# An MLP block on one Trainium2 core: the first w1 block loaded and scaled by halves of its columns, four pairs of x strips opened on it, a warm-up on the identity, two looks moved behind copies

## The chip, the cores and the metric

The kernel runs on one core of a Trainium2 chip. The metric is the device time of one execution in microseconds (us), as the median of several runs. The engines are TensorE (PE in the profile; PEld is its weight load), VectorE (DVE), ScalarE (ACT), GpSimd (POOL) and SyncE (SP), which here only issues transfers. Each engine works its instructions off in its own fixed order and waits for semaphores of the others.

## The reference

```python
# x (8, 1024, 1024), w1 (1024, 4096), w2 (4096, 1024), all float32
h = x @ w1
h = 0.5 * h * (1 + np.tanh(np.sqrt(2 / np.pi) * (h + 0.044715 * h ** 3)))
return (h @ w2).astype(np.float32)
```

## The kernel before, in words

x is taken as 8192 rows of 1024, cut into 64 strips of 128 rows; two strips are a pair (32 pairs). All products run on float16 operands that were scaled first. A strip is loaded (`load_x`), looked at by ScalarE, which sums its absolute values (`look_x`), given a scale by two tiny VectorE instructions (`scale_x`), cast (`cast_x`, on ScalarE, VectorE or GpSimd) and turned: eight 128x128 transposes on TensorE into PSUM, and a copy to the tile `xT` (`turn_x_pe`).

w1 is cut by columns into four blocks r of 2 x 512 columns. A block is a 2 x 2 arrangement of sub-blocks B11, B12, B21, B22 (upper or lower 512 rows; left or right 512 columns, 2048 apart). Each block comes in eight loads n of 512 KB (`load_w1`), two for each sub-block, in the order B11, B21, B12, B22. Each load is looked at for its largest magnitude (`look_w1`: on VectorE a reduction, on ScalarE a sum), `widest_w1` joins the looks, `scale_w1` spreads the result over all partitions with one TensorE transpose (the tile `rows`, L157) and takes its reciprocal, and `cast_w1` casts. Block 0 has two scales of its own before they are joined: NR for its left half (loads 0 to 3), NR + 1 for its right half (loads 4 to 7). `join_w1` and `even_w1` bring the two to one scale later, when block 0 is used in the other form.

The first half of the reference, x @ w1 and the gelu, goes in two forms. The opening of block 0 for the first six pairs is plain: a *quarter* (class `Plain`, `quarter`) is one 128 x 512 piece of h, given by pair k, strip half and column side s, and takes eight TensorE products, four with B11 (or B12) and four with B21 (or B22). There are 24 quarters; their list puts s = 0 of the pairs below OPEN first, then s = 1 of these, then the other pairs. Between the first four and the last four products of a quarter `between(p)` puts the next strip's turn and the looks and casts of what comes next. From then on a pair and block is a *unit* (class `Quad1`) of seven products of half size on sums of sub-blocks (`sum_x`, `sum_w1`), with partial results copied out of PSUM by ScalarE (L503, L513, L522) and added by VectorE. A gelu is one ScalarE activation out of PSUM with a factor per row (`up`), then a multiplication by GpSimd to float16 (L173, tile `g`) and a store to DRAM. The second half, the product with w2, follows with 26 products of 256 columns for each pair; it is untouched.

What sets the order: everything is recorded by hand, engine by engine, in the order of the source (`manual_schedule`); no scheduler moves anything. `plan(u, slot, ...)` puts a background step at a slot of unit u, `early(p, ...)` behind quarter p. The opening itself is written out in lines 793 to 874. Transfers from SP go on one hardware queue and are issued in order, with eight landing semaphores in rotation, so the ninth issue waits until the first has landed. w1 blocks 1 to 3 are loaded on GpSimd's queue, so these issues stand in GpSimd's order between its casts.

The places that the change and the prediction touch: the opening (L793 to L874), `load_w1`, `look_w1`, `widest_w1`, `join_w1`, `even_w1`, `cast_w1` (L267 to L323), `factors_of_block` (L250), `warm_up` (L410), `Out1` with its gelus (L421 to L458), and the plan of block 2's looks (L673 to L676). The opening's sequence before: load x0, w1 loads 0 to 3, x1 to x5, w1 loads 4 to 7, x6, x7; cast and turn x0; 14 warm-up products on the cast x0; looks at loads 0 to 3 (the last shared by VectorE and ScalarE); scale; eight more warm-up products; casts of loads 0 and 1 on VectorE, 2 and 3 on ScalarE; quarters, beginning with pair 0.

Of the kernel before, what the change touches and what calls it, by code (L numbers as in the profile page):

```python
# [8 lines left out]
F32 = mybir.dt.float32  # L9
# [4 lines left out]
P = 128  # L14
TINY = 1e-18
SPAN = 256.0


# [61 lines left out]
def kernel(  # L80
# [23 lines left out]
    LAST = 4  # L104
    OPEN = 3
    WARM = 14
    Q = O // 4
# [19 lines left out]
    w1c = small.tile([P, NR, 12], F32, name="w1c")  # L127
    w1a = small.tile([P, NR + 2], F32, name="w1a")
    w1m = small.tile([P, NR + 2], F32, name="w1m")
    w1i = small.tile([P, NR + 2], F32, name="w1i")  # L130
    w1j = small.tile([P, NR + 2], F32, name="w1j")
# [8 lines left out]
    rt = small.tile([P, T // P], F32, name="rt")  # L140
    up = small.tile([P, 2, 2 * FIRST], F32, name="up")
    ratio = small.tile([P, 2], F32, name="ratio")

# [99 lines left out]
    def factors(k0, k1, r):  # L243
# [4 lines left out]
        times(view(rs), xi[:, c], w1j[:, r:r + 1])  # L248

    def factors_of_block(k, block, eng):  # L250

        c, b = slice(2 * k, 2 * k + 2), slice(NR + block, NR + block + 1)
        times(up[:, block, c], xm[:, c], w1m[:, b], eng)
        times(rt[:, c] if block else rs[:, k, :, 0], xi[:, c], w1j[:, b], eng)

    def factors_of_pair(k):
        for h in range(2):
            times(us[:, k, h, :], w1m[:, :NR], xm[:, 2 * k + h:2 * k + h + 1])
            times(rs[:, k, h, :], w1j[:, :NR], xi[:, 2 * k + h:2 * k + h + 1])
        times(rt[:, 2 * k:2 * k + 2], xi[:, 2 * k:2 * k + 2], w1j[:, NR + 1:NR + 2])  # L260


# [4 lines left out]
    def load_w1(r, n, pool=wpool, tag="w"):  # L267
        b, half = BLOCKS[n // 2], n % 2
        row = (b in (B21, B22)) * HK * P + half * 2 * P
        col = (b in (B12, B22)) * I // 2 + r * N  # L270
        wraw[r, n] = pool.tile([P, 2, N], F32, name="wn", tag=tag)
        (G if r else nc.sync).dma_start(
            out=wraw[r, n],
            in_=w1[row:row + 2 * P, col:col + N].rearrange("(c p) n -> p c n", p=P),
        )

    def look_w1(r, n, eng=V, part=None):

        i = n + 2 * (n // 4) + (2 if part else 0)
        src, dst = wraw[r, n], w1c[:, r, i:i + 1]  # L280
        if part is not None:
            src = src[:, part:part + 1]
        src = src.rearrange("p c n -> p (c n)")
        if eng is S:
            junk = k2.tile([P, 2 * N], mybir.dt.bfloat16, name="junk", tag="k2")
            junk = junk[:, :src.shape[1]]
            S.activation(out=junk, in_=src, func=ACT.Abs, scale=1.0 / SPAN, accum_out=dst)  # L287
        else:
            absmax(dst, src)

    def widest_w1(r, block=None):

        c, src = (r, w1c[:, r, :]) if block is None else (NR + block, w1c[:, r, 6 * block:6 * block + 6])
        V.tensor_reduce(out=w1a[:, c:c + 1], in_=src, op=ALU.max, axis=AX.X)
# [8 lines left out]
    def inverse_w1(c, eng=V):  # L303
        times(w1j[:, c], w1i[:, c], 1.0 / SPAN, eng)

    def join_w1():

        V.tensor_tensor(out=w1m[:, :1], in0=w1m[:, NR:NR + 1], in1=w1m[:, NR + 1:], op=ALU.max)
        V.reciprocal(w1i[:, :1], w1m[:, :1])
        times(ratio, w1m[:, NR:], w1i[:, :1])  # L310
        V.tensor_copy(out=w1j[:, :1], in_=w1j[:, NR:NR + 1])

    def even_w1(b, half):
        t = w1set[0, b][:, 2 * half:2 * half + 2]
        block = b in (B12, B22)
        cast(G, t, t, ratio[:, block:block + 1])

    def cast_w1(r, n, eng):
        b, half = BLOCKS[n // 2], n % 2
        if (r, b) not in w1set:  # L320
            w1set[r, b] = wpool.tile([P, HK, N], F16, name="w", tag="w")
        c = r or NR + n // 4
        cast(eng, w1set[r, b][:, 2 * half:2 * half + 2], wraw.pop((r, n)), w1i[:, c:c + 1])  # L323

# [27 lines left out]
    def scale_w2():  # L352
        all_partitions(w2n, w2a)
        V.tensor_scalar_max(w2n, w2n, TINY)
        V.reciprocal(w2i, w2n)
        V.tensor_scalar(out=w2s, in0=w1m, scalar1=w2i, scalar2=None, op0=ALU.mult)

# [52 lines left out]
    def warm_up(t, n):  # L410
        warm = bank("pb")
        for _ in range(n):
            nc.tensor.matmul(  # L413
                warm[:, :N // 2], lhsT=t[:, :P], rhs=t[:, :N // 2],
                start=True, stop=True, skip_group_check=True,
            )
# [4 lines left out]
    class Out1:  # L421


        def begin(self, k, r):
# [6 lines left out]
            if not r and k < FIRST:  # L431
                self.u = [[up[:, s, c(h)] for s in range(2)] for h in range(2)]
            if k not in gd:
                gd[k] = dram.tile([2 * P, I], F16, name="gd", tag="gd")

        def e(self):
            return k2.tile([P, N], F32, name="e", tag="k2")

        def gelu_pair(self, half, s, src):
            e = self.e()  # L440
            S.activation(out=e, in_=src, func=ACT.Gelu_apprx_tanh, scale=self.u[half][s])
            if half not in self.g:
# [9 lines left out]
        def gelu(self, half, s, e, src):  # L452
            S.activation(out=e, in_=src, func=ACT.Gelu_apprx_tanh, scale=self.u[half][s])  # L453
            g = k1.tile([P, N], F16, name="g", tag="k1")
# [10 lines left out]
    class Plain(Out1):  # L465
        def __init__(self, k, r):
            self.begin(k, r)
            self.g = {}

        def quarter(self, half, s, which, between):  # L470
# [166 lines left out]
    for k in range(OPEN, FIRST):  # L637
        for h in range(2):
            c = 2 * k + h
            p = (6, 9, 12)[k - OPEN] + h  # L640
            early(p - 1, look_x, c)
            early(p, scale_x, c)
            early(p, cast_x, c, V)
            if h:
                early(p, factors_of_block, k, 0, V)
                early(p, factors_of_block, k, 1, G)
            if k > 3:
                early((2, 5)[k - 4], load_x, c, wpool, "w")
            early(4 * k - 2 + 2 * h - (k > 2), turn_x_pe, c, V if h else S)
# [7 lines left out]
    for n in range(8):  # L657
        early((3, 4, 6, 7, 8, 9, 10, 11)[n], load_w1, 1, n)
        early((7, 8, 10, 12, 12, 13, 14, 15)[n], look_w1, 1, n, S if n in (3, 5, 7) else V)
# [9 lines left out]
    for r in range(2, NR):  # L669
        u = (r - 1) * FIRST - 1  # L670
        for n in range(8):
            v = u - 1 + n // 2
            if r == 2:  # L673
                plan(*((4, 1), (4, 3), (5, 0), (5, 2))[n // 2], load_w1, r, n)
                look = ((5, 3), (5, 4), (6, 1), (6, 1), (6, 3), (7, 1), (7, 1), (7, 4))[n]
                plan(*look, look_w1, r, n, S if n % 2 else V)  # L676
# [110 lines left out]
    with tc.manual_schedule(  # L787
# [5 lines left out]
        load_x(0, wpool, "w")  # L793
        for n in range(4):
            load_w1(0, n)
# [4 lines left out]
        V.tensor_copy(out=identity16, in_=identity)  # L800
        for c in range(1, 2 * OPEN):
            load_x(c, wpool, "w")
        for n in range(4, 8):
            load_w1(0, n)
        for c in range(2 * OPEN, 8):
            load_x(c, wpool, "w")
        look_x(0)
        scale_x(0)
        cast_x(0, S)
        t = x16[0]  # L810
        turn_x_pe(0, S)
        warm_up(t, WARM)
        for n in range(3):
            look_w1(0, n)
        look_w1(0, 3, V, 0)
        look_w1(0, 3, S, 1)
        widest_w1(0, 0)
        look_x(1)
        scale_w1(NR)
        warm_up(t, 8)  # L820
        cast_w1(0, 0, V)
        inverse_w1(slice(NR, NR + 1), G)
        cast_w1(0, 1, V)
        cast_w1(0, 2, S)
        cast_w1(0, 3, S)
        scale_x(1)
        cast_x(1, V)
        for c in range(2, 5):
            look_x(c)
        factors_of_block(0, 0, G)  # L830
        plain = {k: Plain(k, 0) for k in range(FIRST)}
        quarters = [(k, 0, half, s) for s in range(2) for k in range(OPEN) for half in range(2)]
        quarters += [(k, 0, half, s) for k in range(OPEN, FIRST) for half in range(2) for s in range(2)]

        def between(p):
            if p == 0:
                turn_x_pe(1, V)
                scale_x(2)
                cast_x(2, V)
            elif p == 1:  # L840
                scale_x(3)
                turn_x_pe(2, V)
                cast_x(3, V)
                look_x(5)
                scale_x(4)
                cast_x(4, V)
                factors_of_block(1, 0, G)
            elif p == 2:
                turn_x_pe(3, V)
                look_w1(0, 4)  # L850
                look_w1(0, 5, S)
            elif p == 3:
                scale_x(5)
                cast_x(5, G)
                turn_x_pe(4, V)
                look_w1(0, 6)
                look_w1(0, 7, S)
                widest_w1(0, 1)
                factors_of_block(2, 0, G)
            elif p == 4:  # L860
                turn_x_pe(5, V)

        for p, (k, r, half, s) in enumerate(quarters):
            plain[k].quarter(half, s, ("pa", "pc")[p % 2], lambda: between(p))
            if p == 4:
                scale_w1(NR + 1)
# [51 lines left out]
```

## Time and profile before

| | |
|---|---|
| median of 3 runs | 1531.62 us (1531.59 to 1531.94) |
| the profiled execution's own time | 1532.23 us |
| its span, first to last instruction | 1530.4 us |
| ScalarE's start on x0 (its landing) | 4.59 us |
| TensorE's first instruction (turn of x0) | 7.36 us |
| TensorE's first product of a quarter | 12.96 us |
| looks at an x strip on ScalarE, first 60 us | 12, mean 1048 ns |
| 128x1024 casts of w on ScalarE, first 60 us | 8, mean 1145 ns |
| gelus of 128x512 out of PSUM (L441) | mean 687 ns |

The profile is of one execution. Its times count from the first instruction; the execution's own time is longer than the span by what lies around it. A timeline gives for each engine start, length and what ran, and in brackets the idle time ahead and what ended it. Products are pipelined, so a group's length has a tail of some 0.16 us that overlaps with the next group: eight products of 512 columns stand in the list with 1.89 us but begin 1.73 us apart from the next eight.

### The profile page before, as it was taken

Reading aid. Unit: us, or ns where it says so; the run is one execution under the profiler, and the core shown is the slowest. Engines: PE = TensorE matmul, PEld = TensorE weight load, DVE = VectorE, ACT = ScalarE, POOL = GpSimd, SP = SyncE. Lnnn points to the kernel's source line nnn. Section 1 sums busy time; section 2 is a strip of 40 time slices with the busy share of each in tenths; the row PEclk is TensorE's granted clock in tenths of the full one; section 3 lists DMA queues with packets and bytes.
Section 4 is the critical chain, followed back from the end, with each engine's and each line's share of the span. In section 5 each row is a group of like instructions: output and inputs, shape, how many; then the busy total and the mean of one; then the engine's idle time right before and its main releaser. Section 6 shows DMA issues by size and latency. Waiting matters only on the chain.

```text
span 1530.4 us, 28624 instructions
## 1 busy us (share of the span) xinstructions
PE 1518.0 (99%) x10388; PEld 1013.0 (66%) x10388; DVE 1179.4 (77%) x2406; ACT 736.5 (48%) x1307; POOL 475.6 (31%) x591
## 2 busy tenths in 40 slices
PE   7999999999999999999999999999999999999999
PEld 4444444444444444444458888888888888888888
DVE  6886788777876777574348888888888888888886
ACT  7878777777777777787662111111111111111111
POOL 5688554555666656554440000000000000000000
PEclk9999999999999999999999999999999999999999
DMA  9664988878778787875995767767866866866873
GB/s 357 230 196 133 299 273 290 253 237 239 213 241 270 220 262 226 252 200 131 285 275 135 144 135 135 144 139 132 156 130 130 163 133 122 163 135 130 150 143 79
DMA packets 459935, 293.94 MB, mean 192 GB/s; under 512 B 333968, under 2 KB 427152, under 8 KB 459792
## 3 DMA queue, kind: packets, MB, share of 16 engines
q1 hardware_dynamic: 456336, 279.52, 71.8%
q0 software_dynamic: 3456, 12.58, 2.5%
q8 instruction: 81, 1.33, 0.4%
q14 instruction: 62, 0.51, 0.1%
HBM read 96.99 MB, written 114.29 MB: 138 GB/s over the span
## 4 chain that ended last, share of the span: by engine, by line
PE 99%; DVE 1%; ACT 0%; DMA 0%; issue 0%; ACTq 0%
PE pa L401 52%; PE pc L401 31%; PE pb L401 14%; PE turned L212 0%; DMA xn<-in_x_dram 0%; DVE x L175 0%; PE pb L413 0%; DVE w L175 0%; DVE xT L219 0%; ACT x L171 0%; ACT junk L186 0%; ACT junk L287 0%; PE rows L157 0%; DVE xi L193 0%; DVE o L571 0%
## 5 line engine op out<-in xcount | busy, mean ns | idle before, releaser
L401 PEld LDWEIGHTS <-gs 128*128 128x128 f16 x4608 | 450.8, 98 | 53.1 <-DVE gs L167 0.2
L173 POOL TENSOR_SCALAR g<-e,rs 128x512 f16<-128x512 f32 x446 | 364.2, 826 | 285.7 <-ACT e L453 248.6
L401 PEld LDWEIGHTS <-xs 128*128 128x128 f16 x1952 | 191.0, 98 | 230.5 <-issue 0.9
L164 DVE TENSOR_TENSOR e<-pc,e 128x512 f32<-128x512 f32 x244 | 162.9, 686 | 204.2 <-ACT e L522 202.8
L401 PEld LDWEIGHTS <-xT 128*128 128x128 f16 x1656 | 161.2, 98 | 194.1 <-DVE xT L219 1.7
L401 PE MATMUL pa<-w,gs 128*128 128x256 f16 x2304 | 288.3, 273 | 0.0
L401 PE MATMUL pa<-w,xT 128*128 128x512 f16 x1072 | 254.4, 379 | 0.4 <-DVE w L175 0.3
L453 ACT ACTIVATE e<-e,us 128x512 f32<-128x512 f32 x366 | 251.2, 719 | 3.1 <-DVE e L164 3.1
L401 PE MATMUL pa<-w,xs 128*128 128x512 f16 x976 | 250.5, 379 | 0.6 <-ACT e L503 0.6
L401 PE MATMUL pc<-w,xs 128*128 128x512 f16 x976 | 250.5, 379 | 0.0
L401 PEld LDWEIGHTS <-gT 128*128 128x128 f16 x2048 | 200.4, 98 | 23.2
L575 ACT ACTIVATE o<-pa,vo 128x256 f32<-128x256 f32 x96 | 45.2, 471 | 332.5 <-PE pa L401 332.5
L401 PE MATMUL pc<-w,gs 128*128 128x256 f16 x1536 | 193.8, 273 | 0.0
L401 PE MATMUL pa<-w,gT 128*128 128x256 f16 x1024 | 132.7, 273 | 0.0
L401 PE MATMUL pb<-w,xT 128*128 128x512 f16 x488 | 125.3, 379 | 0.0
L571 DVE SCALAR_TENSOR_TENSOR o<-pc,vo,o 128x256 f32<-128x256 f32 x160 | 77.1, 482 | 57.8 <-PE pc L401 57.8
L513 ACT COPY e<-pa 128x512 f32<-128x512 f32 x122 | 71.4, 585 | 92.3 <-PE pa L401 83.9
L167 DVE TENSOR_TENSOR gs<-gT,gs 128x1024 f16<-128x1024 f16 x160 | 109.9, 687 | 1.2 <-DMA gT<-gd 1.2
L571 DVE SCALAR_TENSOR_TENSOR o<-pa,vo,o 128x256 f32<-128x256 f32 x192 | 92.2, 481 | 19.5 <-PE pa L401 19.3
L401 PE MATMUL pb<-w,gs 128*128 128x256 f16 x768 | 99.5, 273 | 0.0
L401 PE MATMUL pc<-w,gT 128*128 128x256 f16 x768 | 99.5, 273 | 0.0
L503 ACT COPY e<-pa 128x512 f32<-128x512 f32 x122 | 70.5, 578 | 50.7 <-PE pa L401 50.6
(104 smaller groups left out, 1436.6 us busy)
## 6 DMA issues: line engine op xcount, KB each, us to landing
gd<-g SPq DMA_DIRECT2D x500, 128.0 KB, 3.2
wn<-in_w_dram SPq DMA_DIRECT2D x72, 512.0 KB, 5.4
xn<-in_x_dram SPq DMA_DIRECT2D x64, 512.0 KB, 5.4
out_dram<-o SPq DMA_DIRECT2D x62, 512.0 KB, 4.0
w<-wd SPq DMA_DIRECT2D x25, 512.0 KB, 6.0
wn<-in_w_dram POOLq DMA_DIRECT2D x24, 512.0 KB, 6.3
wd<-wt SPq DMA_DIRECT2D x24, 512.0 KB, 4.2
gT<-gd SPq DMA_TRANSPOSE x128, 6.4
```

The costliest lines, as they stand in the source:

```text
L164: V.tensor_tensor(out=o, in0=a, in1=b, op=ALU.add)
L167: V.tensor_tensor(out=o, in0=a, in1=b, op=ALU.subtract)
L173: G.tensor_scalar(out=o, in0=i, scalar1=s, scalar2=1.0, op0=ALU.mult, op1=ALU.mult)
L401: nc.tensor.matmul(bank, lhsT=left(i), rhs=right[i], start=start and i == 0, stop=i == n - 1, skip_group_check=True,)
L453: S.activation(out=e, in_=src, func=ACT.Gelu_apprx_tanh, scale=self.u[half][s])
L503: S.copy(self.e11, self.pa)
L513: S.copy(self.e12, self.pa)
L571: V.scalar_tensor_tensor(out=o, in0=ps, scalar=v, in1=o, op0=ALU.mult, op1=ALU.add)
L575: S.activation(out=o, in_=ps, func=ACT.Copy, scale=v)
```

## The change

Block 0's first half (B11 and B21) is loaded by halves of its columns: loads 0 and 1 bring columns 0 to 255 of the upper and lower 512 rows (four row groups of 256 columns each), loads 2 and 3 columns 256 to 511. Each half has its own scale (columns NR + 2 and NR + 3 of the scale tiles), so the factor `up` has three versions, and a gelu over both halves is two activations of 256 columns. `join_halves` makes the common maximum for the factor behind the gelu. The first two quarters (pair 0) become four *eighths* of 256 columns; x1 is loaded between load 1 and load 2. OPEN goes from 3 to 4: x6 and x7 are loaded ahead of w1 loads 4 to 7, and s = 0 of four pairs comes ahead of s = 1. The 14 warm-up products on x0 become 52 of 128 columns on the identity ahead of x0's turn, and three ahead of the rows product, eight behind it and three ahead of x1's turn. In the opening x0 is cast by ScalarE as before, x5 and x7 by GpSimd, the others by VectorE; looks at w1 loads 4 and 6 are VectorE's, 5 and 7 ScalarE's, loads 1 and 3 shared, load 2 ScalarE's. Block 1's first two loads are one quarter later. Two of block 2's looks, loads 1 and 3, move in the plan from (5, 4) and (6, 1) to (6, 1) and (6, 4), which is behind the copies of unit 6.

```diff
-    OPEN = 3
-    WARM = 14
+    OPEN = 4
+    WARM = 52
...
+    def ups_of_block(k, eng):
+        c = slice(2 * k, 2 * k + 2)
+        for half in range(2):
+            times(up[:, half, c], xm[:, c], w1m[:, NR + 2 + half:NR + 3 + half], eng)
...
+        c, w = 2, N
+        if not r and n < 4:
+            c, w = HK, N // 2
+            row, col = n % 2 * HK * P, n // 2 * w
...
+    def join_halves():
+
+        V.tensor_tensor(
+            out=w1m[:, NR:NR + 1], in0=w1m[:, NR + 2:NR + 3], in1=w1m[:, NR + 3:], op=ALU.max
+        )
+        V.reciprocal(w1i[:, NR:NR + 1], w1m[:, NR:NR + 1])
...
+        def act(self, half, s, e, src):
+            u = self.u[half][s]
+            u = u if isinstance(u, tuple) else (u,)
+            w = N // len(u)
+            for i, scale in enumerate(u):
+                c = slice(i * w, (i + 1) * w)
+                S.activation(out=e[:, c], in_=src[:, c], func=ACT.Gelu_apprx_tanh, scale=scale)
...
+        def eighth(self, half, part, ps):
+
+            t = xT[self.k]
+            c = slice(part * N // 2, (part + 1) * N // 2)
+            for j, b in enumerate((B11, B21)):
+                product(
+                    ps[:, c], lambda n: t[:, half, j * HK + n, :],
+                    [w1set[0, b][:, n, c] for n in range(HK)], j == 0,
+                )
...
-        early((3, 4, 6, 7, 8, 9, 10, 11)[n], load_w1, 1, n)
+        early((4, 5, 6, 7, 8, 9, 10, 11)[n], load_w1, 1, n)
...
-                look = ((5, 3), (5, 4), (6, 1), (6, 1), (6, 3), (7, 1), (7, 1), (7, 4))[n]
+                look = ((5, 3), (6, 1), (6, 1), (6, 4), (6, 3), (7, 1), (7, 1), (7, 4))[n]
...
         load_x(0, wpool, "w")
-        for n in range(4):
+        for n in range(2):
+            load_w1(0, n)
+        load_x(1, wpool, "w")
+        for n in range(2, 4):
             load_w1(0, n)
...
-        for c in range(1, 2 * OPEN):
+        for c in range(2, 2 * OPEN):
             load_x(c, wpool, "w")
         for n in range(4, 8):
             load_w1(0, n)
-        for c in range(2 * OPEN, 8):
-            load_x(c, wpool, "w")
+        warm_up(identity16, WARM)
         look_x(0)
         scale_x(0)
         cast_x(0, S)
         t = x16[0]
+        look_w1(0, 0)
+        look_w1(0, 1, V, 0)
+        look_w1(0, 1, S, 1)
         turn_x_pe(0, S)
-        warm_up(t, WARM)
...
+        warm_up(t, 3)
+        widest_w1(0, 2)
+        look_x(1)
+        scale_w1(NR + 2)
+        warm_up(t, 8)
+        cast_w1(0, 0, V)
+        cast_w1(0, 1, V)
+        plain = {k: Plain(k, 0) for k in range(FIRST)}
+        pa, pc = bank("pa"), bank("pc")
+        plain[0].eighth(0, 0, pa)
+        look_w1(0, 2, S)
+        scale_x(1)
+        cast_x(1, V)
         look_w1(0, 3, V, 0)
         look_w1(0, 3, S, 1)
+        widest_w1(0, 3)
+        look_x(2)
+        warm_up(t, 3)
+        turn_x_pe(1, V)
+        scale_w1(NR + 3)
+        plain[0].eighth(1, 0, pc)
+        cast_w1(0, 2, V)
+        cast_w1(0, 3, S)
+        ups_of_block(0, G)
+        scale_x(2)
+        cast_x(2, V)
+        look_x(3)
+        join_halves()
+        inverse_w1(slice(NR, NR + 1), G)
+        plain[0].eighth(0, 1, pa)
+        turn_x_pe(2, V)
+        times(rs[:, 0, :, 0], xi[:, 0:2], w1j[:, NR:NR + 1], G)
+        plain[0].gelu(0, 0, plain[0].e(), pa)
+        look_x(4)
+        plain[0].eighth(1, 1, pc)
+        plain[0].gelu(1, 0, plain[0].e(), pc)
+        scale_x(3)
+        cast_x(3, V)
...
+            if p == 2:
+                turn_x_pe(3, V)
                 look_x(5)
                 scale_x(4)
                 cast_x(4, V)
                 factors_of_block(1, 0, G)
...
             elif p == 3:
+                turn_x_pe(4, V)
+                look_x(6)
+                look_x(7)
                 scale_x(5)
                 cast_x(5, G)
...
+                look_w1(0, 4)
             elif p == 4:
                 turn_x_pe(5, V)
+                scale_x(6)
+                cast_x(6, V)
+                factors_of_block(2, 0, V)
+                look_w1(0, 5, S)
+                look_w1(0, 7, S)
+            elif p == 5:
+                turn_x_pe(6, V)
+                scale_x(7)
+                cast_x(7, G)
+                look_w1(0, 6)
+                widest_w1(0, 1)
+            elif p == 6:
+                turn_x_pe(7, V)
+                factors_of_block(3, 0, V)
```

## Prediction

> **What bounds it now.** I read the page first, then TensorE's timeline and its waits in the first 80 us, then the chain of waits in order of time, then the other engines' timelines over the same stretch. The span is TensorE's work behind a head of 13 us.
>
> ```profile
> PE 1518.0 (99%) x10388; PEld 1013.0 (66%) x10388; DVE 1179.4 (77%) x2406; ACT 736.5 (48%) x1307; POOL 475.6 (31%) x591
> ...
> PE 99%; DVE 1%; ACT 0%; DMA 0%; issue 0%; ACTq 0%
> ```
>
> So only two things can change the time: when TensorE's useful work begins, and how long it then stands still. TensorE's timeline (start, length, what):
>
> ```profile
> 8.19 3.19 PE L413 MATMUL pb<-x 128*128 128x256 f16 x14
> 11.17 0.42 PE L157 MATMUL rows<-identity,w1a 128*128 128x128 f32 x1
> 11.44 1.24 PE L413 MATMUL pb<-x 128*128 128x256 f16 x8
> 12.96 1.25 PE L401 MATMUL pa<-w,xT 128*128 128x512 f16 x4 [0.28 <-DVE w L175]
> 14.68 0.62 PE L212 MATMUL turned<-identity,x 128*128 128x128 f16 x8 [0.46 <-DVE x L175]
> ...
> 31.07 1.89 PE L401 MATMUL pa<-w,xT 128*128 128x512 f16 x8
> ```
>
> L413 is warm-up; the first product starts at 12.96. The ninth quarter (s = 1, pair 0) starts at 31.07. Between lie 8 quarters of 8 x 0.216 = 1.73 us, 5 turns of 0.45 (8 transposes at 0.056) and a rows product, 0.11: 16.2 of 18.1 us, so 1.9 us of stalls. After 31.07 the engine is gapless but for 0.16 at 42.9 and one stall, which the waits (PE behind ACT e L503, 0.6) and ScalarE's timeline explain:
>
> ```profile
> 62.51 1.05 ACT L287 ACTIVATE junk<-wn 128x1024 bf16<-128x1024 f32 x1
> 63.45 0.19 ACT L287 ACTIVATION_READ_ACCUMULATOR junk<-wn 128x1 f32 x1
> 63.55 0.57 ACT L503 COPY e<-pa 128x512 f32<-128x512 f32 x1
> ```
> ```profile
> 62.52 1.03 PE L401 MATMUL pb<-w,xT 128*128 128x512 f16 x4
> 64.17 1.02 PE L401 MATMUL pa<-w,xs 128*128 128x512 f16 x4 [0.62 <-ACT e L503]
> ```
>
> The product at 64.17 was due at 62.52 + 0.86 = 63.39: 0.78 us lost, because a look at a w1 block stood ahead of the copy.
>
> **Part 1, the first product.** Unchanged: x0 lands at 4.57, its look, scale and cast end at 7.31. Six loads in, the trace's records of landing are 4.57, 5.89, 7.27, 8.62, 9.95, 11.23: 1.28 us per x strip (4 KB rows), 1.35 per w1 load (2 KB rows). The new w1 loads have the same bytes in 1 KB rows. The nearest 1 KB rows are the stores of g, 0.33 us apart for 128 KB behind each other, so 1.33 per 512 KB; a cost per packet, as from 1.28 to 1.35, would give 1.48. I take 1.37. Landing then: w 5.9 and 7.3, x1 8.6, w 9.95 and 11.3. The second load's half look on VectorE (0.69) ends at 8.0, on ScalarE behind cast x0 (0.63 + 0.19) at 8.05; widest 0.16; rows at 8.2. From rows to cast it took 0.83 (25.74 to 26.57), the cast 0.75: first product at **9.85, 3.1 us earlier**; the second half of it behind the second cast (0.67 on) at 10.5.
>
> **Part 2, the second half block.** ScalarE: copy xT of x0 to 9.05, look x1 to 10.2, look w to 11.2, half look to 11.95. VectorE: scale and cast x1 10.45 to 11.55 (0.38 + 0.75), half look to 12.15, widest 12.3, copy xT of x1 12.25 to 12.85, and w1m behind it; cast w from 13.4 to 14.15. ScalarE's cast waits behind look x2 (lands 12.55, done 13.6) and ends 14.7. TensorE: product 2 at 12.95, product 3 at 14.2 and 14.75, turn x2 15.2, product 4 15.65 to 16.55. At this state (two quarters, x1 and x2 turned) before stood at 18.5: 1.9 ahead.
>
> **Part 3, quarters 2 to 6.** Between two turns TensorE has 1.73 us; VectorE needs copy 0.61, scale 0.38, cast 0.75 and some 0.25 to and from PSUM: 2.0. So each turn waits about 0.2 (before: 0.17 to 0.34), and x5, cast on GpSimd in 1.12, about 0.55. Turns: x3 17.65, x4 20.05, x5 22.8, x6 25.15; TensorE is ready for x7 at 27.3.
>
> **Part 4, where x7 stands.** Its cast is on GpSimd, in order behind g of quarter 4 and the issue of the load of w1 block 1. That g waits for quarter 4's gelu, and ScalarE's order has looks at w1 loads 5 and 7 ahead of this gelu. Load 7 is now the last of the 16 first loads, which x7 was before (landing on record: 24.30); with four loads 0.02 longer, 24.4. What each step behind takes:
>
> ```profile
> 21.85 1.06 ACT L287 ACTIVATE junk<-wn 128x1024 bf16<-128x1024 f32 x1
> ```
> ```profile
> 22.77 1.12 POOL L173 TENSOR_SCALAR x<-xn,xi 128x1024 f16<-128x1024 f32 x1
> ...
> 24.51 0.69 POOL L173 TENSOR_SCALAR g<-e,rs 128x512 f16<-128x512 f32 x1
> 25.14 0.89 POOL L272 DMA_DIRECT2D wn<-in_w_dram  x1
> ```
>
> Look 24.4 to 25.45 (next start 1.04 on); two half gelus; no row has them. A 512 copy from PSUM took 0.578, a 256 one with a scale 0.471, a 512 gelu 0.687; 0.687 less 256 columns at 0.83 ns is 0.474, the second starting 0.38 behind the first (between 0.29, half the present pitch, and 0.57, no shorter than a whole one): to 26.3. g from 26.35, issue 0.64 on, cast 0.80 behind it (29.85 to 30.65 at the next issue): 27.8 to 28.95. **Turn x7 at 29.0, a new stall of 1.7.** Then 0.45, half a quarter 0.86, rows 0.11, quarter 7 1.73: the ninth quarter at 32.15. Before, 31.07 plus the turns of x6 and x7, which it does later, 2 x 0.45: 31.97. **The head ends 0.2 us behind**; all 3.1 are given back.
>
> **Part 5, the rest.** The two looks of block 2 go behind copies: the copy starts when its product ends, 61.66 + 1.03 = 62.69 on the old clock, and ends 63.26, ahead of 63.39. Next late is the copy behind the moved look (1.04 from 63.26, so 64.3; its product ends 64.4): no stall. **Minus 0.78** (0.6 to 0.78). The casts of w1 loads 5 to 7 end 32.45, 33.05 and 33.5 against needs of 32.6, 33.0 and 33.45: plus 0.1 (0 to 0.3). The 0.16 at 42.9 may go; I take 0. At nothing: twelve gelus in halves (0.18 each) under ScalarE's 52% idle time, the extra up factors (0.26 on GpSimd, 0.15 on VectorE), evening by columns (as many elements as before), GpSimd's loads of block 1 one slot later (looked at from about 33, landing about 33.5, used from 50). 52 warm-ups begin behind the identity's cast (1.6), at 0.107 end at 7.15, before x0.
>
> Sum: 0.2 - 0.78 + 0.1 = -0.5. The profiled execution took 1532.23 (span 1530.4 and 1.8 around it), so 1531.7; the median of the runs is 0.6 below it: **1531.1**.
>
> **The clock.** Before, products of 256 columns stand 0.213 apart until 11.8 us, 4.4 us after the first transpose at 7.36, then 0.109; the page's PEclk shows 9 throughout, so I go by spacing. New warm-ups start at 1.6, so 4.4 later is 6.0, before x0 is turned. Released after that, x0's turn and three warm-ups cost up to 0.4 + 0.3 more, rows come 0.6 later, and about 0.45 reaches the end. The Trainium skill, TensorE: Matmul & The Clock Gate, Part 1, says that the window of about 3.4 us is free-running, so that release falls anywhere from one to two windows after the start; by that it is estimated at 5.0 to 8.4, and the sum by its late end is 1531.55.
>
> **Rivals.**
> A: x7 is not held (the look at load 7 ends early, or g overtakes), so the stall is as at x5, 0.55: 1.15 better, and the half us of slack in Part 3 may count: 1529.6. For it: all upstream steps are ready. Against: every queue is in order. 0.13.
> B, slower: 1 KB rows move more slowly, and load 7 lands late. Place: ScalarE's look at load 7. Behind it each us is a us of the end, so the balance turns at a landing of 24.9. At 1.48 a load it is 24.85 (1531.55), at 1.7 25.75: 1532.4. For: 4 KB to 2 KB already costs 5%. Against: the stores of g. The Trainium skill, DMA: Bandwidth & Descriptors, Specifications, puts line rate at transfers from 512 B on; by that the landing is 24.3 and the sum 1531.0. 0.18.
> C, the warm-up on the identity does not do what it says, or the clock falls back: from 8.2 to 16.5 TensorE is busy some 60%. Not released until 11.8, as before: rows product about 0.9 and first product 1.6 later than at 9.85, about 1.1 at the end: 1532.2; falling back for one stretch of 3.4 us half-paced: 1.7, 1532.8. Against: before, 12.4 to 16.1 was busy 60% too, and its transposes stood 0.056 apart. 0.13.
>
> **Chances.** Forecast 0.51 (1530.5 to 1531.9), A 0.13, B 0.18, C 0.13, 0.05 for what I don't see. Range 1530.2 to 1533.0: it leaves out most of A and the far ends of B and C. 0.2% is 3.1 us, about what a measurement of this kernel can tell from no change. No case reaches it alone: faster 0.03 (A with all stalls of Part 3 gone), same 0.94, slower 0.03 (B and C together).
>
> **What would show it.** First product near 9.85, product 4 ending near 16.5; PE turned waiting near 27.3 to 29.0 with GpSimd's cast of x as releaser, behind an ACT look released by the DMA of wn; no PE wait on ACT e near 64. Wrong, if the turn of x7 starts before 28, if transposes at 7.4 stand 0.107 apart, or if the w1 loads land over 1.5 us apart.

## The result and the profile after

After: **1533.68 us** (median of 22 runs, 1532.97 to 1535.27) against 1531.84 before (22 runs, 1531.31 to 1532.32). The ratio is 1.0014, 95% interval 1.0007 to 1.002: slower by 1.8 us, 2.6 above the 1531.1 that was forecast and outside the range. The profiled execution of after took 1533.54, its span is 1531.8 (before 1532.23 and 1530.4).

On the page of after, the engine totals look as they did before. In the chain of work that ended last, DMA has 2% instead of 0, and GpSimd's `x`, its `wn` issue and its `g` are new, each below half a per cent.

```profile
PE 1521.4 (99%) x10449; PEld 1017.0 (66%) x10449; DVE 1180.4 (77%) x2417; ACT 740.0 (48%) x1321; POOL 473.9 (31%) x592
...
PE 98%; DMA 2%; POOL 0%; SPq 0%; DVE 0%; issue 0%
```

TensorE's timeline of after (start, length, what; idle time and its releaser in brackets):

```profile
1.64 4.96 PE L451 MATMUL pb<-identity 128*128 128x128 f16 x52 [1.64 <-DVE identity L858]
7.61 0.62 PE L213 MATMUL turned<-identity,x 128*128 128x128 f16 x8 [1.01 <-ACT x L172]
8.06 0.49 PE L451 MATMUL pb<-x 128*128 128x256 f16 x3
8.82 0.29 PE L158 MATMUL rows<-identity,w1a 128*128 128x128 f32 x1 [0.26 <-DVE w1a L312]
...
10.48 1.26 PE L438 MATMUL pa<-w,xT 128*128 128x256 f16 x8
...
16.39 1.04 PE L438 MATMUL pc<-w,xT 128*128 128x256 f16 x8
...
24.02 0.62 PE L213 MATMUL turned<-identity,x 128*128 128x128 f16 x8 [0.44 <-POOL x L174]
...
27.94 1.04 PE L438 MATMUL pa<-w,xT 128*128 128x512 f16 x4
30.99 0.62 PE L213 MATMUL turned<-identity,x 128*128 128x128 f16 x8 [2.02 <-POOL x L174]
...
34.15 1.98 PE L438 MATMUL pa<-w,xT 128*128 128x512 f16 x8
```

The reader sees the forecast's shape with other sizes. The first product starts 2.5 us before its old place (12.96), product 4 at 16.39, and TensorE is ready for x7 at 28.80 (27.94 and four products of 0.216). Then it stands still for 2.2 us (2.02 behind the modelled end of the last product). The ninth quarter starts at 34.15, where before it stood at 31.97 with as much work done: the head ends **2.2 us later**. From there to the end after needs 1531.8 - 34.15 = 1497.65, before 1530.4 - 31.97 = 1498.43: **about 0.8 less**, the size at which the two moved looks were priced (what it consists of stands under Part 5 below). 2.2 - 0.8 is the 1.4 by which the spans differ.

What held x7 is the chain of waits of after from 25 us on (start, length, what):

```profile
20.89 7.33 DMA gd<-g
28.22 0.01 issue
28.23 0.69 POOL g L174
28.93 0.84 POOL wn L286
29.76 0.05 issue
29.81 1.13 POOL x L174
30.95 0.05 issue
30.99 0.62 PE turned L213 x8
```

and ahead of it ScalarE's timeline of after:

```profile
26.26 1.06 ACT L302 ACTIVATE junk<-wn 128x1024 bf16<-128x1024 f32 x1 [1.29 <-DMA wn<-in_w_dram]
27.23 0.19 ACT L302 ACTIVATION_READ_ACCUMULATOR junk<-wn 128x1 f32 x1
27.32 0.82 ACT L483 ACTIVATE e<-pa,up 128x256 f32<-128x256 f32 x2
```

ScalarE waits 1.29 us for the last w1 load, looks at it, does the gelu of quarter 4; GpSimd does its g, issues a load, casts x7. All six steps are the forecast's, in its order. Load 7 landed at 26.18, not at 24.4. The first row of the chain names another releaser for this g, the store of an earlier one. It is the gelu, as the run with the looks later (below) shows: there the gelu ends at 27.25 and g starts at 27.34, 0.09 behind it as in after (28.14, 28.23), while the records of landing of that store come at 27.59 to 29.31.

**Why the last of the 16 lands 1.9 later than before's last.** The records of landing of the first 16 loads, in us:

| | x0 lands | first four w1 loads, each | 2 KB w1 loads | x strips | largest gap between two | last of the 16 |
|---|---|---|---|---|---|---|
| before | 4.57 | 1.32 to 1.38 (2 KB rows) | 1.35 to 1.36 | 1.26 to 1.29 | 1.38 | 24.30 |
| after | 4.81 | 1.41 to 1.50 (1 KB rows) | 1.31 to 1.37 | 1.27 to 1.33 | **2.43**, x5 to x6 | 26.18 |

So 0.24 are a later start (of this execution alone: in the other twelve profiles x0 lands at 4.34 to 4.62), about 0.45 are the 1 KB rows (four times 0.11), and 1.15 are one gap in front of x6 (2.43 less 1.28), which lands at 19.5. In that gap the transfers of after, from 16.5 to 17.5 us, show a queue other than the loads' (packets, MB, share of the time of 16 engines):

```profile
q1 hardware_dynamic: 104, 0.39, 96.9%
q8 instruction: 1, 0.02, 6.8%
```

One packet of 16 KB, with 6.8% of 16 engine-microseconds: it holds one of the 16 DMA engines for 1.09 us, from 16.71 on. It is TensorE fetching its next stretch of program, as the count below shows. The trace has sixteen records of landing for each load, and a load has landed with the last of them. Up to x5 the last comes at most 0.04 behind the one before it; from x6 to load 7 it comes 1.14 to 1.19 behind: fifteen of load 7's sixteen stand by 25.01, the last at 26.18. So one share of everything behind this packet is some 1.15 us late, and the other fifteen lose nothing. Before, the same fetch came at 25.0, when all 16 loads had landed, and no such lag is in their records (0.08 at most). The fetches follow the count of instructions: 81 packets on this queue for 20,898 products and weight loads of the page, one in 258; in each of the thirteen traces the median distance from one packet to the next is 253 to 260 of them. Some 220 to 245 of them are on record ahead of this fetch, in before by 25.0 and in after by 16.7: after issues 44 more warm-ups and, in place of two quarters, twice as many products of half the width, each with its weight load.

### The profile page after: what moved, and what is told of

Read it like the earlier page. It is cut to its first block, busy times and chain, and to the rows that moved or that the text cites. A ratio compares the mean times of both kernels' runs of the same rounds, so it can differ in the third digit from the quotient of the medians.

```text
span 1531.8 us, 28775 instructions
## 1 busy us (share of the span) xinstructions
PE 1521.4 (99%) x10449; PEld 1017.0 (66%) x10449; DVE 1180.4 (77%) x2417; ACT 740.0 (48%) x1321; POOL 473.9 (31%) x592
## 3 DMA queue, kind: packets, MB, share of 16 engines
q8 instruction: 81, 1.33, 0.4%
## 4 chain that ended last, share of the span: by engine, by line
PE 98%; DMA 2%; POOL 0%; SPq 0%; DVE 0%; issue 0%
PE pa L438 52%; PE pc L438 31%; PE pb L438 14%; DMA xn<-in_x_dram 1%; DMA gd<-g 0%; PE turned L213 0%; POOL x L174 0%; SPq L286 0%; POOL wn L286 0%; PE rows L158 0%; POOL g L174 0%; DVE o L627 0%; SPq L183 0%; SPq L504 0%
## 5 line engine op out<-in xcount | busy, mean ns | idle before, releaser
L438 PE MATMUL pa<-w,xT 128*128 128x512 f16 (+1 forms) x1080 | 254.8, 377 | 0.3
```

The costliest lines, as they stand in the source:

```text
L438: nc.tensor.matmul(bank, lhsT=left(i), rhs=right[i], start=start and i == 0, stop=i == n - 1, skip_group_check=True,)
```

## The experiments

Each kernel was timed in 11 runs beside 27 to 33 runs of before in the same batch; before's median was 1531.61, 1531.62 and 1531.66 in the three batches.

### Taking links out of the chain of x7

**The looks at loads 5 and 7 behind the gelu of quarter 4** (after, with this edit):

```diff
         elif p == 4:
-            look_w1(0, 5, S)
-            look_w1(0, 7, S)
         elif p == 5:
             ...
             cast_x(7, G)
             look_w1(0, 6)
+            look_w1(0, 5, S)
+            look_w1(0, 7, S)
```

> The changed kernel, but ScalarE's looks at w1 loads 5 and 7 stand one quarter later, behind the gelu of quarter 4. Theory (load 7 lands at 26.2 and holds ScalarE, and through it gelu, GpSimd's g, its load issue and the cast and turn of x7): the gelu no longer waits for the landing; next late are its factors, which VectorE writes behind the cast of x6 (26.4 to 26.75 in the changed kernel's trace), so it starts at 26.8 instead of 27.3 and x7's turn moves from 31.0 to 30.4: 0.55 us faster than the changed kernel, median 1533.1. Rival (the landing only happens to fall there, GpSimd's own queue is late): turn of x7 stays at 31.0, 1533.7. If the landing alone were the hold and nothing came next, the turn would come at 29.0 to 29.6 and the median at 1531.9.

Measured: 1533.30 (1532.31 to 1534.02), ratio 1.0011 (1.0002 to 1.002). Turn of x7 in its TensorE timeline:

```profile
30.10 0.62 PE L213 MATMUL turned<-identity,x 128*128 128x128 f16 x8 [1.44 <-POOL x L174]
```

The stall falls from 2.2 to 1.6, not to nothing: the look is one gate of quarter 4's gelu, and the next one is 0.6 us earlier, VectorE's factors of pair 2 behind the cast of x6. The forecast had only the first. (The turn is 0.9 earlier than in after; 0.3 of it is that TensorE was ready earlier, in an execution in which x0 landed at 4.38 and not at 4.81.)

**x7 cast on VectorE instead of GpSimd** (`cast_x(7, G)` to `cast_x(7, V)` in after):

> The changed kernel, but x7 is cast by VectorE instead of GpSimd, so that its turn waits for nothing of ScalarE's and GpSimd's queues. Theory: VectorE has x7's scale at 28.15, cast to 28.95, turn at 29.0 instead of 31.0; the stall of 2.0 goes but for 0.2, and the median comes to 1531.7 to 1531.9, the same as the kernel before. The look at load 6 starts 0.7 later and its result is still ahead of the rows product. Rival (something else, such as the scale of the right half behind load 7, takes the place): the ninth quarter moves less than 1 us and the median stays above 1532.8. Clock: if the stall of 2 us is what lets the clock fall back in the slower of the changed kernel's executions (granted clock 0.999 there), no execution shows 0.999 here; if the thin stretch from 8 to 16 us is, about a quarter of them still do.

Measured: 1533.05 (1531.80 to 1533.50), ratio 1.0007 (0.9998 to 1.0016). The stall at x7 falls from 2.2 to 0.6, but its TensorE and VectorE timelines show the next thing that is late:

```profile
29.78 0.62 PE L213 MATMUL turned<-identity,x 128*128 128x128 f16 x8 [0.44 <-DVE x L176]
...
32.13 1.90 PE L438 MATMUL pc<-w,xT 128*128 128x512 f16 x8 [0.58 <-DVE xT L220]
33.87 1.99 PE L438 MATMUL pa<-w,xT 128*128 128x512 f16 x8
```
```profile
28.54 1.18 DVE L176 TENSOR_SCALAR x<-xn,xi 128x1024 f16<-128x1024 f32 x1
29.64 1.20 DVE L151 TENSOR_REDUCE w1c<-wn 128x1 f32<-128x1024 f32 x1
30.95 0.16 DVE L312 TENSOR_REDUCE w1a<-w1c 128x1 f32<-128x6 f32 x1
31.38 0.69 DVE L220 COPY xT<-turned 128x1024 f16<-128x1024 f16 x1 [0.27 <-PE pa L438]
```

VectorE now casts x7 in 1.18 (0.75 for x6), and the copy of x7 stands behind the look at load 6 and the join. Half of the rival: something else took the wait's place, though a smaller one.

**x7 cast one quarter earlier on GpSimd**, ahead of quarter 4's g and of the load's issue:

```diff
         elif p == 4:
             cast_x(6, V)
+            scale_x(7)
+            cast_x(7, G)
             factors_of_block(2, 0, V)
             ...
         elif p == 5:
             turn_x_pe(6, V)
-            scale_x(7)
-            cast_x(7, G)
```

> The kernel after, with the scale and the cast of x7 put one quarter earlier, so that GpSimd casts x7 ahead of quarter 4's g and of the load's issue, and nothing of x7 waits for load 7; the looks stay. Theory (the turn of x7 waits for load 7 only through the order of three queues; all upstream steps are ready): GpSimd casts x7 from about 26.8 to 27.95, TensorE takes the turn when it is ready, near 28.8, with no wait over 0.3; the ninth quarter starts near 32.0 instead of 34.15, the span is about 1529.6, the median about 1531.2, some 0.5 under the kernel before beside it. Rival (the landing of load 7 itself is the bound, whatever the queues): rows or the casts of loads 4 to 7 take the wait over, the ninth quarter stays later than 33.3, and the median is above 1532.5.

Measured: 1531.84 (1531.42 to 1532.90), ratio 1.0001 (0.9992 to 1.001): the loss is gone. TensorE, then VectorE:

```profile
28.60 1.04 PE L438 MATMUL pa<-w,xT 128*128 128x512 f16 x4 [0.62 <-DVE xT L220]
29.48 0.61 PE L213 MATMUL turned<-identity,x 128*128 128x128 f16 x8
...
32.62 2.05 PE L438 MATMUL pa<-w,xT 128*128 128x512 f16 x8
```
```profile
26.86 1.10 DVE L242 TENSOR_SCALAR rs<-xi,w1j 128x2 f32<-128x2 f32 x1
27.87 0.68 DVE L220 COPY xT<-turned 128x1024 f16<-128x1024 f16 x1
```

x7 is turned without a wait, as the theory says; load 7 lands as late as ever (26.48) and the time no longer shows it, against the rival. But the ninth quarter stands at 32.62 and not at 32.0: a new wait of 0.6 for the copy of x6, because a product of 128x2 numbers ahead of it took 1.10 us (0.22 in after). It ends, at 27.96, with GpSimd's cast of x7 (26.79 to 27.94).

**Both, x7 ahead and the looks later:**

> As the run with x7 cast ahead, and the looks at loads 5 and 7 behind the gelu of quarter 4 as well. Theory: with x7 out of the queue, the gelu of quarter 4 has nobody who waits for it before its bank is wanted again, so this adds nothing: within 0.3 of the other run, ninth quarter near 32.0. Rival: the late gelu still holds a bank or a factor, and this is better by 0.5 or more.

Measured: 1532.30 (1531.96 to 1533.53), ratio 1.0005 (0.9996 to 1.0014). Both sides missed: it is 0.5 worse than x7 ahead alone. The looks, now later on ScalarE, end at 29.8 and hold `widest_w1` by 0.21, and again a small VectorE step beside GpSimd's g takes 0.79 (0.35 in after); the casts of loads 4 to 7 begin at 32.00 (31.74 there).

**x7 ahead, and the factors of pair 2 moved into VectorE's gap before the copy of x5** (against the run with x7 ahead):

```diff
         elif p == 3:
             look_w1(0, 4)
+            factors_of_block(2, 0, V)
         elif p == 4:
             ...
             cast_x(7, G)
-            factors_of_block(2, 0, V)
```

> The kernel after with x7 cast a quarter earlier, and with the factors of pair 2 put on VectorE into the gap ahead of the copy of x5 (there it stood idle 0.8 us), so that the copy of x6 isn't behind a 1.10 us multiplication of two columns beside GpSimd's cast. Theory: the 0.6 us wait for the copy of x6 goes, the ninth quarter starts near 32.0 (32.62 in the run without this step), where before it was 31.97: the head has then gained nothing, and the median is 0.6 below that run, about 1531.2 to 1531.4, which is before less most of the 0.78 of the two looks. Rival (the wait moves on again, to the casts of loads 4 to 7 or to the gelus): ninth quarter at 32.4 or later, median 1531.7 or above.

Measured: 1531.46 (1531.09 to 1531.87), ratio 0.9999 (0.999 to 1.0008). TensorE:

```profile
27.70 1.04 PE L438 MATMUL pa<-w,xT 128*128 128x512 f16 x4
28.58 0.61 PE L213 MATMUL turned<-identity,x 128*128 128x128 f16 x8
...
31.92 2.12 PE L438 MATMUL pa<-w,xT 128*128 128x512 f16 x8
```

Both waits are gone and the ninth quarter starts at 31.92, before's 31.97: with no stall left at x7, the whole new opening is worth nothing that the traces show (0.05 us), and what remains of the change is the two looks (the profiled span is 1529.5, 0.9 under before's). The medians say less: 1531.46 is only 0.20 below before's 1531.66 of its batch, where the two looks alone gain 0.76 (below). So by the medians this opening still costs some 0.5 us that no profiled execution shows; that is within the intervals of both, and what it is stays open.

### The parts alone, on the kernel before

**The two looks** (before, with only the changed `look` line of the plan):

> The kernel before with one part of the change alone: block 2's looks at loads 1 and 3 behind the copies. Theory: TensorE's stall of 0.78 at 64 goes and nothing is late next: median 0.8 below the kernel before, 1531.05. Rival (the moved look holds the next copy): at most 0.3 faster.

Measured: 1530.85 (1530.64 to 1531.65), against 1531.61: 0.76 less, and the wait behind ScalarE's `e` is not in its list of TensorE's waits (engine, line, for whom; us in total, times, longest):

```profile
PE turned L212 <- ACT x L171: 7.2, 1, 7.2
PE rows L157 <- DVE w1a L294: 1.3, 1, 1.3
PE pa L401 <- DVE w L175: 0.5, 1, 0.5
PE turned L212 <- DVE x L175: 0.5, 1, 0.5
```

The ratio's interval, 0.9986 to 1.0004, holds 1, so the time alone doesn't prove it; what speaks for it is that the wait is gone from the trace and that the size fits. This is the fastest kernel of the study.

**The warm-up on the identity** (before, with 52 warm-ups on the identity, and 3 instead of 14 on x0):

> The kernel before with another part alone: 52 warm-up products on the identity ahead of x0's turn, three behind it instead of 14. Theory: the clock is granted at about 5.6 instead of 11.9, the rows product no longer stands behind warm-up (from 11.17 to 10.95) and is followed faster, first product 12.55 instead of 12.96; 0.2 to 0.45 faster, 1531.4 to 1531.65. Code loading: TensorE's instructions are used up faster by some 54, so its 16 KB instruction load, at 25.0 before, falls into the first loads (near 19 to 21), takes about 1 us of one DMA engine, and the x strips loaded last land about 1.1 later, without reaching the end because nothing waits for them. Rival (the 1.2 us hole in the changed kernel's landings has another cause, such as the 1 KB rows): landings as before, the last at 24.3.

Measured: 1532.30 (1532.07 to 1532.84), ratio 1.0004 (0.9995 to 1.0013); the mean granted clock is 0.998 or 0.999 in all 11 runs. It is 0.7 slower than before's 1531.61 where 0.2 to 0.45 faster was expected. TensorE, and the busy time of each engine in stretches of it, where the column behind POOL is the granted clock:

```profile
7.68 0.49 PE L414 MATMUL pb<-x 128*128 128x256 f16 x3
11.31 0.44 PE L157 MATMUL rows<-identity,w1a 128*128 128x128 f32 x1 [3.14 <-DVE w1a L294]
11.55 1.91 PE L414 MATMUL pb<-x 128*128 128x256 f16 x8
13.26 1.91 PE L401 MATMUL pa<-w,xT 128*128 128x512 f16 x4
```
```profile
9.00:10.50 1.50, 0.00 (x0) 0.00 (x0) 1.38 (x2) 0.30 (x1) 0.00 (x0) 1.00 1.06 419
10.50:14.00 3.50, 2.69 (x11) 1.68 (x12) 2.64 (x8) 2.94 (x6) 0.85 (x2) 0.51 1.03 416
```

The clock was released at 7.1, fell back at 10.55 in the idle stretch and came back at 17.4: the first product runs at half pace (its first four in 1.91, where before's take 1.25). The second thing to see needs no row of 1 KB: TensorE's fetch moved here too, from 25.0 to 18.56 (by 41 more products with their weight loads, not the 54 of the expectation), and the load that lands behind it comes 2.79 after the one before it, the last at 25.83 instead of 24.30.

**The same with the two looks and 26 warm-ups on x0**, so that TensorE is busy up to the rows product:

> The kernel before with the two looks moved, 52 warm-ups on the identity, and 26 warm-ups behind the turn of x0 instead of 3, so that TensorE is busy up to the rows product. Theory (the clock fell back in the run with 3 because TensorE stood idle for 3.1 us, and a code load in the stretch of the first loads delays only what lands last, which this kernel does not want before 33): the clock stays released from about 6, first product near 12.7 (before 12.96), last load about 25.5 instead of 24.3 and nobody waits for it; median 0.2 under the kernel with the two looks alone, about 1530.6. Rival (the clock falls back whatever the filling, or the late load costs the head): first product past 13, median at 1531.5 or more.

Measured: 1531.16 (1530.71 to 1532.12), ratio 0.9997 (0.9988 to 1.0006). Clock 1.0 in all 11 runs, first product at 12.86. TensorE's fetch at 15.15, a gap of 2.45 between two loads behind it, the last load at 25.75; no wait of TensorE for it is in the trace. Filled, the clock holds. The 0.2 expected on top of the two looks is not there: the kernel is 0.46 below before's 1531.62 of its batch, the two looks alone were 0.76 below theirs, a difference within the intervals of both.

**The 1 KB rows** (before, with the first four w1 loads as halves of columns):

```diff
+        if not r and n < 4:
+            c, w = HK, N // 2
+            row, col = n // 2 * HK * P, n % 2 * w
```

> The kernel before with one thing of the change: the first four w1 loads are halves of columns in 1 KB rows (same bytes, same casts, looks and scale, one block). Theory (the form of the rows alone makes a load slower: 1.46 in the trace of after against 1.345): each of these four loads lands 1.45 to 1.48 behind the one before, the fourth at about 10.4 instead of 9.95, the first product starts about 0.45 later, near 13.4, the last x lands at about 24.75, the median is 0.4 above the kernel before. Rival (the slower pace in after comes from something else in it, the warm-ups or the order of issue): loads 1.35 apart, first product near 12.96, no difference.

Measured: 1532.27 (1531.86 to 1533.55), ratio 1.0006 (0.9997 to 1.0015). The loads land 1.48 to 1.51 apart, the fourth at 10.35, the last x at 24.73; TensorE's fetch stays at 24.9 and there is no gap. So rows of 1 KB are enough for the slow pace. They are not needed for it: beside the warm-ups on the identity the first four loads of 2 KB rows came 1.34 to 1.54 apart as well (the two runs above), and what slows those stays open. The price of the rows isn't settled by this run: the first product waits here for the casts of both column halves (13.87, 0.9 late), and yet the ninth quarter's place, 30.93 (31.07 before), isn't late at all in the profiled execution.

### Is TensorE early for nothing? And once more after

**After without its 14 warm-ups between the turn of x0 and the fourth product:**

> The kernel after without its 14 warm-ups between the turn of x0 and the fourth product. Theory (load 7 sets the head's end; TensorE is ready for x7 some 2 us too soon): even if the clock falls back for a stretch between 8 and 17, TensorE loses up to 1.7 us there and the turn of x7 starts within 0.4 of where it did (31.0): median within 0.5 of the kernel after (1533.3 or so). Rival (the clock's fall-back adds to the end, as in the executions with a granted clock of 0.999): 1534.3 to 1535.2.

Measured: 1534.19 (1533.43 to 1534.58), ratio 1.0016 (1.0007 to 1.0024), clock 0.998 or 0.999 in every run. Stretches with the granted clock, then TensorE's timeline:

```profile
9.00:10.50 1.50, 0.29 (x1) 0.23 (x2) 0.97 (x3) 1.50 (x2) 0.00 (x0) 0.65 1.10 370
10.50:14.00 3.50, 3.14 (x17) 1.96 (x16) 3.08 (x8) 2.40 (x7) 0.27 (x1) 0.50 1.05 400
```
```profile
28.84 1.04 PE L438 MATMUL pa<-w,xT 128*128 128x512 f16 x4
31.30 0.62 PE L213 MATMUL turned<-identity,x 128*128 128x128 f16 x8 [1.42 <-POOL x L174]
```

Half pace from 9.4 to 16.3 makes TensorE ready for x7 0.9 later than in after, and the turn starts 0.3 later: the stall hides the rest, as the theory says. The median is 0.5 above after's 1533.68 (0.2 above the 1534.00 below), at the edge of what the theory allows.

**After once more, beside the two kernels above:**

> The kernel after once more, beside the other two on the same chip, as their measure. Theory (load 7 lands near 26.2 in every execution, and the turn of x7 waits for it through the queues): median 1533.1 to 1533.8, turn of x7 between 30.7 and 31.3, code load of TensorE between 16 and 17.5. Rival (the late landing is an accident of the one profiled execution): turn of x7 before 30.0.

Measured: 1534.00 (1533.31 to 1534.91), ratio 1.0016 (1.0007 to 1.0025); turn of x7 at 31.18 behind a wait of 1.77, fetch at 16.98, a gap of 2.28, load 7 at 26.39. The median is 0.2 above the range that was expected, the rest inside it. The late landing is no accident: in eight profiled kernels with the new opening it lies between 26.12 and 26.48.

## Why the prediction was wrong

The mechanism was right and one term of the sum was mis-sized: **Part 4's landing of load 7**, forecast at 24.4 and measured at 26.18, which put the end of the head 2.0 us later than forecast. The other 0.7 of the miss is the step from the span to the median (last point).

- **Part 4.** Forecast 24.4, measured 26.18. Behind it the steps cost what was forecast: look to gelu 1.06 (1.05), gelu to g 0.91 (0.90), g to issue 0.64 (0.64), issue to cast 0.94 (0.80), cast to turn 1.18 (1.2). The turn comes at 30.99 instead of 29.0 and the ninth quarter at 34.15 instead of 32.15: 2.0 of the error, 1.78 of it the landing, one for one as rival B said of its place. Rival B's cause was the lesser part: the 1 KB rows take 0.11 a load more than before's (1.37 forecast, 1.41 to 1.50 measured; its own upper end, 1.48, was right) and put load 7 about 0.45 behind, 0.36 of it not forecast. The Trainium skill, DMA: Bandwidth & Descriptors, Specifications, has transfers from 512 B on at line rate; here rows of 1 KB take 1.50 us per 512 KB, of 2 KB 1.35 and of 4 KB 1.28. The 1.15 of the program fetch were in no term and no rival, and neither was the later start of 0.24.
- **What could have been seen.** The fetches are a row of before's page, too, and one stands at 25.0 in its transfers, just behind the last of the 16 loads. Counting the TensorE instructions that the change adds ahead of it would have put it among them.
- **Part 1.** First product 10.48 for 9.85. Rows to product 1.66 (1.65 forecast); the 0.6 stand ahead of the rows product, in landings: x0 0.24, load 1 at 7.69 for 7.3.
- **Part 2.** Product 4 starts at 16.39 for 15.65: the same 0.7, carried on. **Part 3.** Turn of x5 behind a wait of 0.44 (0.55 forecast); turn to turn 2.46, 2.88 and 2.51 for 2.4, 2.75 and 2.35, which makes it 1.5 late when TensorE is ready for x7. With x7 set free (28.58 in the run with the factors moved), the ninth quarter starts at 31.92, level with before's 31.97 and not 1 us ahead, as rival A had it (32.15 less 1.15): A's price failed by 0.9 although that run has no stall at x7 at all. Without any stall the forecast would be 32.15 less 1.7, 30.45, so the drift of Parts 1 to 3 comes to 1.5. (In before the ninth quarter is one of pair 1 and not of pair 0, since three pairs are opened there; the count of eight quarters ahead of it is right.)
- **Part 5.** The looks are right: 0.78 forecast, 0.76 alone, and TensorE's wait at 64 is gone in after. The 0.8 that after gains behind the head is a net of more: the 0.16 at 42.9 is gone too, and 0.25 is lost at 53, where the rows product of block 1 waits for the look at that block's last load (0.6 in after again). The prediction put the later loads of block 1 at nothing.
- **The clock.** Products of 128 columns stand 0.107 apart up to 5.56 and 0.056 from 5.65 on: released some 0.4 ahead of the 6.0 forecast, and held in the profiled execution. That it is so near is partly luck: in the ten profiled executions with these 52 warm-ups, which all begin at 1.6, the record of the granted clock rises anywhere from 4.38 to 7.14, and three of the ten come ahead of the 5.0 to 8.4 that the prediction gave beside it. Rival C comes true in a part of them: 8 of 33 runs of after have a mean granted clock of 0.999. In the first 22 runs they are six, at 1533.93 to 1535.27, where the median of the others is 1533.56; in the 11 later ones 1534.24 and 1534.91, where it is 1533.98. None of the 55 runs of the five kernels with a shorter stall at x7 has it. That the stall of 2 us itself lets the clock fall, behind which nothing hides it, fits; no profile caught one, so it is argued and not shown. Against it as the only way: one run of before with the 1 KB rows, which has no such stall, stands at 0.999 too (1533.55).
- **From span to median.** Before's profiled execution was 0.4 above its median of 22 runs, after's 0.1 below: together with the 0.6 that I had subtracted, this is the rest, some 0.7, of the 2.6.

## What to carry to other kernels

When a change adds instructions ahead of a stretch that waits on loads, count them: TensorE's program comes over the same DMA engines as the loads, and here the fetch moved with the count. An engine that starts earlier gains only as far as the last link of the head allows, so follow the load that lands last through every queue behind it before pricing a start; here three queues in order turned a transfer that is 1.8 late into 2.0 us. And try the small part that seems to pay by itself (the two looks) alone.

## What the runs showed of the hardware

- A TensorE program fetch of 16 KB took 1.08 to 1.13 us on one DMA engine in the early stretch, and made the landing behind it 0.7 to 1.7 late in each of the ten profiled executions in which it fell among the first loads. In the three in which it fell behind them no such gap stands.
- The clock fell back 2.4 us into an idle stretch of 3.1 us (before with the warm-up on the identity) and also where no idle stretch was longer than 1.4 us (after without fill). Both times it fell 3.41 us after its release, with TensorE's records covering 1.0 and 1.7 of these, and stayed at half for 6.83 us. The Trainium skill, TensorE: Matmul & The Clock Gate, Part 1, puts the fall behind an idle window of about 3.4 us; both runs show that a partly idle one is enough.
- VectorE beside GpSimd: 128x2 numbers took 1.10 instead of 0.22 and ended with GpSimd's cast, a 128x1024 cast beside its g 1.18 instead of 0.75. The Trainium skill, SBUF — State Buffer, "SBUF: two separate sides", has a port pair that the two hold exclusively for a whole instruction; the first of these rows agrees.
- In four of the thirteen traces (before with the two looks; after with x7 on VectorE, without fill, and again) the second w1 load landed 2.0 to 2.6 behind the first instead of 1.4 to 1.6, with no fetch beside it. From there on the last of each load's sixteen records lags the one before it by 0.3 to 0.8. In the run with the two looks single packets of the loads took 1.45 and 1.00 us there; what held them stays open.
